# Moving a layer's mixing, transposes and key search to other places in the queues of one core: a streaming encoder step on Trainium2

## The chip, the cores and the metric

The kernel runs on one core of one Trainium2 chip. TensorE (PE) multiplies, VectorE (DVE), ScalarE (ACT) and GpSimd (POOL) work on what it leaves, and SyncE (SP) issues nearly all DMAs from one queue, in order. The metric is the time of one execution in device microseconds.

## What is computed

One layer of a hybrid encoder, for a prompt of 1024 rows and a sample of 32 rows with a cache of 256. Cut to what matters here:

```python
h = rms_norm(x, norm1_g) * (1 + sc1) + sh1
q, k, v, qi, ki, wi, u, vg = jnp.split(h @ w_in, SPLIT_POINTS, axis=-1)
q, k = rope(rms_norm(q, q_norm_g), pos), rope(rms_norm(k, k_norm_g), pos)   # 8 heads x 64
s = jnp.einsum('bqhd,bsd->bqhs', qi, ki)                                     # the indexer
score = jnp.einsum('bqhs,bqh->bqs', jax.nn.relu(s), wi)
score = jnp.where(mask[None], score, -jnp.inf)
top_val, top_idx = lax.top_k(score, topk)       # 256 keys for each query (sample: 72)
...                                             # softmax attention over the chosen keys
u = jax.nn.gelu(u)
vn = layer_norm(jax.nn.gelu(vg), gmlp_ln_g, gmlp_ln_b)
gm = u * (ws_m @ vn + bs)                       # chunks of 128 rows
y = jnp.concatenate([attn, gm], axis=-1) @ w_out
x = x + g1 * y
h2 = rms_norm(x, norm2_g) * (1 + sc2) + sh2
x = x + g2 * (jnp.square(jax.nn.relu(h2 @ w_ff1)) @ w_ff2)
```

## The kernel before

The rows are cut into eight blocks of 128 and one of 32 (the sample, NB). Products are made in three passes over operands split into a rounded part and a rest. The work comes in stages.

First `ada` makes shifts, scales and gates, x is normalised and transposed, and the index columns of w_in are multiplied (`zgroup` with `post_idx`). `score_block` gives each block from 2 on, and the sample, a row of scores for each query.

Then five more column groups of 512 are multiplied, each by one `zgroup`: four pairs of blocks, 48 products of 512 columns (line 313) to a pair, and after each pair a `post_` function. They come in the order q, vg, u, k, v. `post_q` and `post_k` normalise and rotate (`norm_rope`; the rotation, `rope`, is on POOL) and store q and k to DRAM. `post_vg` ends with the mixing product (`mixp`, line 502), which PE reads from a tile that POOL has just written. `post_u` multiplies on POOL and ends with four transposes (`gmt`, line 512). During v, `keys` loads k back and `stack_k` transposes it (`kst`, line 348) and splits it on ACT and DVE. A bank that these steps use comes from a ring of two (`tp`).

Beside these groups runs the search for the 256th largest score of each query (`find_top`): 31 steps, each of which counts the scores above a threshold, bit by bit, and a last part that marks the chosen keys (lines 594 to 610). Two searches are on DVE: `tb` for blocks 2 and 3, `tc` for blocks 5, 4 and NB. Two count on ACT: `ta` for block 7 and `td` for block 6. A step on ACT counts there (line 569), and POOL makes the next threshold in two small operations (lines 570 and 571). All four searches stand in the program before the group v.

`attention` then works on one block at a time, in the order 0, 2, 1, 3, 4, 5, NB, 6, 7. q is loaded from DRAM into `qn` with each head doubled, PE transposes it (`qst`, line 360), and ACT and DVE split it into `qs`. For each head follow the logits (`lgp`, line 690), a DVE operation that adds the mask and takes the minimum (line 691), exp on ACT, a scaling on POOL, transposes (`ppt`) and the product with v (`pv`). After it come w_out (`wo`), the second norm and the feed-forward part (`ff1`, `ff2`), and `emit` stores y, turned by DVE's transposes of 32 x 32 squares, in four DMAs to a piece.

What sets the order: the program is written in the order above, and a scheduler then orders each engine's instructions by simulated times and places tiles in rings. Each engine then runs its queue strictly in that order.

## Time and profile before

| | us |
|---|---|
| median of 3 runs | 1486.31 (1480.2 to 1489.41) |
| the profiled execution | 1479.71 |
| its span, first to last instruction | 1478.0 |
| PE busy | 1380.9 (93%) |
| DVE busy | 843.5 (57%) |
| ACT busy | 528.8 (36%) |
| POOL busy | 550.0 (37%) |

The busy shares are means over stages with different limits, so they say little by themselves. From the trace: the index stage ends near 118 us, attention's first logits start at 469 us, its last product ends near 624 us, the feed-forward part runs from 725 us, and the last product of all ends near 1466 us.

### The profile page before, as it was taken

Reading aid. Unit: us, or ns where it says so; the run is one execution under the profiler, and the core shown is the slowest. Engines: PE = TensorE matmul, PEld = TensorE weight load, DVE = VectorE, ACT = ScalarE, POOL = GpSimd, SP = SyncE. Lnnn points to the kernel's source line nnn. Section 1 sums busy time; section 2 is a strip of 40 time slices with the busy share of each in tenths; the row PEclk is TensorE's granted clock in tenths of the full one; section 3 lists DMA queues with packets and bytes.
Section 4 is the critical chain, followed back from the end, with each engine's and each line's share of the span. In section 5 each row is a group of like instructions: output and inputs, shape, how many; then the busy total and the mean of one; then the engine's idle time right before and its main releaser. Section 6 shows DMA issues by size and latency. Waiting matters only on the chain.

```text
span 1478.0 us, 23705 instructions
## 1 busy us (share of the span) xinstructions
PE 1380.9 (93%) x8792; PEld 1244.5 (84%) x8792; DVE 843.5 (57%) x1987; ACT 528.8 (36%) x1114; POOL 550.0 (37%) x831
## 2 busy tenths in 40 slices
PE   5789797888799999989999999999999999999996
PEld 1767576655467877889999999999999999999996
DVE  1789999999374876532773444334443344433433
ACT  2653346665645765412542111221122211222110
POOL 1656778767950433312342112221122211222120
PEclk9999898999999999999999999999999999999998
DMA  9211111256364221282101111111111111111126
GB/s 363 75 53 47 58 54 51 75 171 234 124 245 115 62 70 64 36 139 73 58 29 49 52 44 44 43 50 51 44 43 44 56 46 44 43 43 57 44 30 89
DMA packets 179947, 114.98 MB, mean 78 GB/s; under 512 B 93412, under 2 KB 147640, under 8 KB 179320
## 3 DMA queue, kind: packets, MB, share of 16 engines
q1 hardware_dynamic: 179832, 113.47, 27.1%
q8 instruction: 69, 1.13, 0.3%
q14 instruction: 46, 0.38, 0.1%
HBM read 97.97 MB, written 15.47 MB: 77 GB/s over the span
## 4 chain that ended last, share of the span: by engine, by line
PE 68%; DVE 17%; POOL 5%; issue 4%; SPq 3%; ACT 2%; DMA 2%; DVEq 0%; POOLq 0%; ACTq 0%
PE f L855 25%; PE f L885 22%; PE wo L836 6%; DVE tcjk L542 4%; PE pv L715 3%; PE lgp L690 3%; PE z L313 3%; PE ppt L702 3%; DVE tbjk L542 2%; SPq L872 2%; POOL tdsm L571 1%; PE ada L154 1%; DVE tcsm L582 1%; DVE sc_b L379 1%; PE qst L360 1%
## 5 line engine op out<-in xcount | busy, mean ns | idle before, releaser
L885 PE MATMUL f<-hid,w 128*128 128x352 f32 x2304 | 372.0, 322 | 0.0
L855 PE MATMUL f<-hh,w 128*128 128x352 f32 x2304 | 371.9, 322 | 0.0
L885 PEld LDWEIGHTS f<-hid,w 128*128 128x128 f32 x2304 | 369.9, 188 | 0.0
L855 PEld LDWEIGHTS f<-hh,w 128*128 128x128 f32 x2304 | 369.1, 188 | 0.0
L775 DVE SCALAR_TENSOR_TENSOR x<-f,mod,x 128x352 f32<-128x352 f32 (+1 forms) x480 | 222.2, 489 | 238.3 <-PE f L885 236.7
L313 PE MATMUL z<-wsp,h 128*128 128x512 f32 (+1 forms) x1152 | 284.0, 397 | 12.9 <-DVE ssh L424 4.4
L860 POOL TENSOR_TENSOR rel<-rel 128x352 f32<-128x352 f32 x96 | 83.6, 872 | 512.4 <-ACT hid L859 512.4
L313 PEld LDWEIGHTS z<-wsp,h 128*128 128x128 f32 x1152 | 213.3, 197 | 71.5 <-issue 12.8
L782 ACT CAST w<-w2r 128x1024 fp32r<-128x1024 f32 x32 | 33.6, 1049 | 283.1 <-PE f L885 272.8
L783 DVE TENSOR_TENSOR w<-w1r,w 128x1024 fp32r<-128x1024 f32 x32 | 39.8, 1245 | 136.3 <-ACT w L782 136.2
L857 ACT ACTIVATE rel<-f 128x352 f32<-128x352 f32 x96 | 44.4, 462 | 153.3 <-PE f L855 152.9
L861 POOL TENSOR_TENSOR hid<-rel,hid 128x352 fp32r<-128x352 f32 x96 | 92.3, 963 | 6.9
L695 POOL TENSOR_SCALAR lg<-lg,ast 128x128 f32<-128x128 f32 (+8 forms) x72 | 51.6, 719 | 97.4 <-DVE ast L694 74.2
L782 ACT CAST w<-w1r 128x1024 fp32r<-128x1024 f32 x32 | 33.5, 1047 | 86.2 <-PE f L855 73.8
L690 PE MATMUL lgp<-kst,qs 128*128 128x256 f32 (+1 forms) x336 | 61.8, 308 | 2.6 <-ACT qs L362 2.5
L195 POOL TENSOR_TENSOR wsp<-wraw,wsp 128x512 fp32r<-128x512 f32 (+1 forms) x44 | 55.5, 1272 | 17.9 <-ACT wsp L194 16.3
L783 DVE TENSOR_TENSOR w<-w2r,w 128x1024 fp32r<-128x1024 f32 x32 | 39.0, 1220 | 37.1 <-ACT w L782 37.1
L692 ACT ACTIVATE lg<-lg,ast 128x128 f32<-128x128 f32 (+8 forms) x72 | 53.9, 750 | 15.3 <-DVE ast L691 10.7
L542 DVE TENSOR_SCALAR_CACHE_REDUCE tcjk<-ya,tcsm 128x768 bf16<-128x768 int16 (+1 forms) x64 | 57.9, 942 | 0.9
L715 PE MATMUL pv<-pT,v 128*64 128x128 f32 (+2 forms) x624 | 57.7, 278 | 0.0
L836 PE MATMUL wo<-gm,wo 128*128 128x352 f32 x288 | 51.9, 329 | 5.1 <-ACT wo L782 5.1
L690 PEld LDWEIGHTS lgp<-kst,qs 128*128 128x128 f32 (+1 forms) x336 | 45.1, 188 | 10.9 <-issue 7.0
(344 smaller groups left out, 1757.5 us busy)
## 6 DMA issues: line engine op xcount, KB each, us to landing
wada<-in_w_ada_dram SPq DMA_DIRECT2D x24, 1024.0 KB, 6.4
w1r<-in_w_ff_dram SPq DMA_DIRECT2D x32, 512.0 KB, 4.0
w2r<-in_w_ff_dram SPq DMA_DIRECT2D x32, 512.0 KB, 3.7
wraw<-in_w_in_dram SPq DMA_DIRECT2D x40, 256.0 KB, 2.9
gm<-gmd SPq DMA_DIRECT2D x4, 1056.0 KB, 5.7
x<-in_x_prompt_dram SPq DMA_DIRECT2D x4, 1024.0 KB, 9.8
gmd<-gmt SPq DMA_DIRECT2D x8, 512.0 KB, 3.6
qn<-qd SPq DMA_DIRECT2D x8, 512.0 KB, 4.7
```

The costliest lines, as they stand in the source:

```text
L313: nc.tensor.matmul(p[:m, :n], h[b][:, k, x, :], w[k][:, y, :], start=k == 0 and q == 0, stop=k == KT - 1 and q == 2)
L542: nc.vector.tensor_scalar(jk[:, :ncol[j]], src, val, None, op0=op, op1=OP.add, accum_out=cnt[:, j:j + 1])
L690: nc.tensor.matmul(ps[:m, d:d + kk.shape[1]], x, kk, start=q == 0, stop=q == 1)
L715: nc.tensor.matmul(ps[64 * j:64 * j + 64, :m], vv, pts[j][:w, k, :m], start=k == 0, stop=k == len(kts) - 1)
L775: nc.vector.scalar_tensor_tensor(y, ps[:, a:a + n], mod[:, 8 * part + k, s:s + 1], y, op0=OP.mult, op1=OP.add)
L782: nc.scalar.copy(ws[:, 0], raw)
L783: eng.tensor_tensor(ws[:, 1], raw, ws[:, 0].bitcast(F32), op=OP.subtract)
L836: nc.tensor.matmul(ps[:, :CW], ws[n][:, x, k, :], mix_at(k, c)[:, y, :], start=k == KO[0] and q == 0, stop=k == KO[-1] and q == 2)
L855: nc.tensor.matmul(ps[:, :CW], ws[n][:, x, k, :], h2_at(k, c)[:, y, :], start=k == 0 and q == 0, stop=k == KT - 1 and q == 2)
L860: nc.gpsimd.tensor_tensor(r, r, r, op=OP.mult)
L861: nc.gpsimd.tensor_tensor(hid[n][:, 1, c * CW:(c + 1) * CW], r, hi.bitcast(F32), op=OP.subtract)
L885: nc.tensor.matmul(ps[:, :CW], w[g][:, x, k, nn * P:(nn + 1) * P], hids[GH * g + k][:, y, c * CW:(c + 1) * CW], start=(g, k) == ks[0] and ...
```

## The change

`zgroup` now keeps a list, `later`. The mixing products, the `gmt` transposes and the key transposes are put on it and made by `settle`, which runs when the products of the next pair are written. The groups come in the order k, q, vg, u, v. After each pair, `advance` lets each search go a given number of steps, held behind the instruction that DVE and ACT had reached two pairs before (in attention: at the block before). The search of blocks 2 and 3 runs in k and q, `tc` starts after k and ends in the group u, and ACT's two searches take 28 of their 31 steps by the end of v and the last 3 in attention. ACT makes its own thresholds, with two small activations instead of POOL's two operations. `norm_rope` squares into SBUF, not in place in the bank.

Attention runs in the order 3, 0, 2, 1, 4, 5, NB, 6, 7. q is loaded by four DMAs in pieces of 32 numbers, so that DVE's transpose of 32 x 32 squares turns it; PE's `qst` transposes are gone. There are four banks for logits and five tiles of them, before three and six. For w_out the weights stand ahead of the rows of x. The last pieces of y use tiles of their own, and every second DMA of theirs goes out from ACT.

```diff
@@ zgroup
+    def settle():
+        while later:
+            later.pop(0)()
...
+    def advance(*pace, back=2):
+        gates.append(gate())
+        g = gates[max(0, len(gates) - back)]
+        with tc.issue_after(g[0]), tc.issue_after(g[1]):
+            for act in (0, 1):
+                for _ in range(pace[act]):
+                    for f in [f for f in searches if f[0] == act][:1 + act]:
+                        if next(f[1], "end") is not None:
+                            searches.remove(f)
...
+            settle()
             post([(b, t0, m, p) for p, (b, t0, m) in zip(ps, g)])
             for b in jobs[j] if jobs else ():
                 keys(b)
+            if pace:
+                advance(*pace[j])
@@ norm_rope, keys, post_vg, post_u
-            nc.scalar.activation(ps[:m], ps[:m], AF.Square)
-            nc.vector.tensor_reduce(ss[:m, e * NH:(e + 1) * NH], heads(ps[:m]), AX.X, OP.add)
+            nc.scalar.activation(t2[:m], ps[:m], AF.Square)
+            nc.vector.tensor_reduce(ss[:m, e * NH:(e + 1) * NH], heads(t2[:m]), AX.X, OP.add)
...
-            stack_k(kt[:, :, d * P:(d + 1) * P], k[d], P, NH)
+            later.append(partial(stack_k, kt[:, :, d * P:(d + 1) * P], k[d], P, NH))
...
+            later.append(partial(mix, b, m, v))
...
+        later.append(partial(gate_out, b, t0, m, x))
@@ find_top
-                        nc.gpsimd.tensor_scalar(dr[:, j:j + 1], cna[:, j:j + 1], ka[:, j:j + 1], 2.0 ** bit, op0=OP.is_lt, op1=OP.mult)
-                        nc.gpsimd.tensor_scalar(t1[:, j:j + 1], t0[:, j:j + 1], dr[:, j:j + 1], -2.0 ** (bit - 1), op0=OP.add, op1=OP.add)
+                        nc.scalar.activation(dr[:, j:j + 1], cna[:, j:j + 1], AF.Sign, bias=ka[:, j:j + 1], scale=-1.0)
+                        nc.scalar.activation(t1[:, j:j + 1], dr[:, j:j + 1], AF.Identity, bias=t0[:, j:j + 1], scale=2.0 ** (bit - 1))
@@ the groups
-    zgroup(zweights(CQ, 512), 512, post_q)
-    zgroup(zweights(CG, 512), 512, post_vg)
-    zgroup(zweights(CU, 512), 512, each(post_u))
...
-    zgroup(wn_, 512, post_k)
...
-    while searches:
-        searches = [f for f in searches if next(f, "end") is None]
+    zgroup(wn_, 512, post_k, pace=4 * ((4, 1),))
...
+    zgroup(wn_, 512, post_q, pace=4 * ((5, 2),))
+    zgroup(zweights(CG, 512), 512, post_vg, pace=4 * ((4, 2),))
+    zgroup(zweights(CU, 512), 512, each(post_u), pace=4 * ((4, 2),))
...
+    zgroup(wv, 512, each(post_v), {0: (4, 0), 1: (1,), 2: (2, 5), 3: (3,)}, pace=((9, 2), (9, 1), (9, 1), (0, 0)))
@@ attention
-        qn = slot([P, D], F32, "qn")
-        nc.sync.dma_start(qn[:m].rearrange("p (a s c) -> p a s c", a=NH, s=2), twice(heads(qd[t0:t0 + m]), m, NH))
+        qn = slot([P, 2, NH, P], F32, "qn")[:, :, :, :m]
+        for q in range(4):
+            d = 32 * (q % 2)
+            nc.sync.dma_start(qn[32 * q:32 * q + 32, 0].rearrange("a h (j b) -> a h j b", b=32), qd[t0:t0 + m].rearrange("(j a) (h c) -> a h j c", a=32, c=HD)[:, :, :, d:d + 32])
...
-        stack_q(qn[:m], m, NH, qs)
+        nc.vector.transpose(qn[:, 1], qn[:, 0])
+        nc.scalar.copy(qs[:, :, 0, :m], qn[:, 1])
+        nc.vector.tensor_tensor(qs[:, :, 1, :m], qn[:, 1], qs[:, :, 0, :m].bitcast(F32), op=OP.subtract)
...
-    for b in (0, 2, 1, 3, 4, 5, NB, 6, 7):
+    for b, pace in ((3, (9, 1)), (0, (9, 1)), (2, (9, 1)), (1, (99, 1)), (4, (0, 2)), (5, (0, 99)), (NB, None), (6, None), (7, None)):
         attention(b)
+        if pace:
+            advance(*pace, back=1)
@@ w_out, emit
+        ws = {n: wsplit(i["w_out"][0, :, n * P:(n + 1) * P], "(k p) c -> p k c", KT, P, "wo", nc.vector if n in (0, 2) else nc.gpsimd) for n in ns}
         for n in ns:
             x_rows(n)
-        ws = {n: wsplit(i["w_out"][0, :, n * P:(n + 1) * P], "(k p) c -> p k c", KT, P, "wo", nc.vector if n in (0, 2) else nc.gpsimd) for n in ns}
...
+            ot = wn.tile([P, CW], F32, name="ot", tag="NS", bufs=2)
...
+            (nc.scalar if q % 2 and c is not None else nc.sync).dma_start(d, s)
```

What PE has queued in the group vg, before, around the mixing products of blocks 2 and 3 (their normalised rows are vg_2092 and vg_2093; h4 to h7 are the inputs of blocks 4 to 7):

```order
L313 MATMUL z_2141<-wsp_1894,h5_446 128x512 x3
L313 MATMUL z_2240<-wsp_1831,h6_471 128x512 x3
L313 MATMUL z_2241<-wsp_1831,h7_496 128x512 x3
L313 MATMUL z_2240<-wsp_1840,h6_471 128x512
L502 MATMUL mixp_2120<-vg_2092,wsT_119 128x128 x4
L502 MATMUL mixp_2131<-vg_2093,wsT_119 128x128 x4
L313 MATMUL z_2240<-wsp_1840,h6_471 128x512 x2
```

And in the changed program, the same two mixing products (now vg_2910 and vg_2911, line 539):

```order
L341 MATMUL z_3121<-wsp_2658,h7_499 128x512 x3
L341 MATMUL z_3120<-wsp_2667,h6_474 128x512 x3
L341 MATMUL z_3121<-wsp_2667,h7_499 128x512
L539 MATMUL mixp_3026<-vg_2910,wsT_122 128x128 x4
L539 MATMUL mixp_3035<-vg_2911,wsT_122 128x128 x4
L341 MATMUL z_3121<-wsp_2667,h7_499 128x512 x2
```

They moved from the first ten products of the pair after the next one to its last eight.

What DVE has queued where attention begins, before (qs is the split q of a block, line 691 the masking of one head's logits, kst the split of the transposed keys):

```order
L353 TENSOR_TENSOR kst_4632<-kst,kst_4632 64x4x128 x4
L363 TENSOR_TENSOR qs<-qst,qs 128x4x128
L691 ISA lg,ast<-lgp,sc_c,rq 128x128
L691 ISA ast 128x1
L691 ISA lg,ast<-lgp,sc_c,rq 128x128
L691 ISA ast 128x1
```

And in the changed program:

```order
L705 STREAM_TRANSPOSE qn<-qn 128x1024
L386 TENSOR_TENSOR kst_4247<-kst,kst_4247 64x4x128 x4
L386 TENSOR_TENSOR kst_4348<-kst,kst_4348 64x4x128 x2
L707 TENSOR_TENSOR qs<-qn,qs 128x8x128
L386 TENSOR_TENSOR kst_4348<-kst,kst_4348 64x4x128 x2
L729 ISA lg,ast<-lgp,sc_b,rq 128x512
L729 ISA ast 128x1
L705 STREAM_TRANSPOSE qn<-qn 128x1024
L729 ISA lg,ast<-lgp,sc_b,rq 128x512
```

The transpose for the second block (the second line 705) now stands behind one masking operation of the first block, and the seven others of that block stand behind it.

What SP has queued behind attention's loads, before (gm are the gated rows, xc the rows of x, wor a third of the weights that `wo` needs first):

```order
L743 DMA gm_6784<-gmd 128x2112
L767 DMA xc<-in_x_prompt_dram 32x32x32 x4
L767 DMA xc<-in_x_sample_dram 32x32 x4
L767 DMA xc<-in_x_prompt_dram 32x32x32 x4
L767 DMA xc<-in_x_sample_dram 32x32 x4
L767 DMA xc<-in_x_prompt_dram 32x32x32 x4
L767 DMA xc<-in_x_sample_dram 32x32 x4
L779 DMA wor<-in_w_out_dram 128x8x128
```

And in the changed program:

```order
L783 DMA gm_6472<-gmd 128x2112
L808 DMA xc<-in_x_prompt_dram 32x32x32 x4
L808 DMA xc<-in_x_sample_dram 32x32 x2
L820 DMA wor<-in_w_out_dram 128x8x128
L808 DMA xc<-in_x_sample_dram 32x32 x2
```

The weights moved from behind 24 loads of x to behind six.

## Rows read from the trace of the kernel before

**Rows 1.** Windows by stage: length, each engine's busy time (instructions), PE clock, DMA.

```profile
118.00:200.00 82.00, 70.78 (x346) 54.37 (x345) 80.07 (x224) 33.97 (x78) 57.18 (x111) 0.94 0.20 63
200.00:280.00 80.00, 67.92 (x360) 54.19 (x359) 74.83 (x198) 47.40 (x120) 61.84 (x141) 0.91 0.17 54
280.00:360.00 80.00, 66.36 (x356) 44.66 (x354) 77.37 (x219) 50.75 (x95) 51.97 (x102) 0.91 0.52 163
360.00:440.00 80.00, 70.58 (x379) 46.45 (x376) 47.43 (x83) 37.65 (x75) 65.10 (x102) 0.91 0.57 196
440.00:469.00 29.00, 25.61 (x130) 20.95 (x128) 12.59 (x21) 13.53 (x25) 0.54 (x4) 1.00 0.32 87
469.00:509.00 40.00, 39.61 (x296) 31.80 (x296) 31.57 (x129) 31.36 (x98) 15.75 (x31) 0.96 0.42 93
509.00:624.00 115.00, 114.96 (x1079) 91.67 (x1078) 80.33 (x259) 65.40 (x162) 37.04 (x43) 1.00 0.21 58
```

**Rows 2.** Chain that ended last, 355 to 470: start, duration, what.

```profile
359.93 8.39 POOL tdsm L571
...
424.65 1.29 DVE tajk L542 x2
...
439.24 1.28 DVE kst L353 x2
...
443.11 6.84 PE z L313 x30
...
469.12 1.34 PE lgp L690 x4
```

**Rows 3.** PE's groups of instructions, 118 to 466: busy, mean ns, idle before.

```profile
L154 PE MATMUL ada<-wada,silu 128*32 128x512 f32 x128 | 20.2, 705 | 0.0
...
L502 PE MATMUL mixp<-vg,wsT 128*128 128x128 f32 (+1 forms) x72 | 14.0, 361 | 10.2 <-POOL vg L497 10.2
...
L348 PE MATMUL kst<-ident,kr 128*128 128x128 f32 (+1 forms) x44 | 6.1, 277 | 1.8 <-DVE kst L353 1.0 <-DMA kr<-out_dram 0.8
```

**Rows 4.** DVE's and POOL's groups of instructions, 118 to 469.

```profile
L428 DVE TENSOR_TENSOR kz<-kz 128x512 f32<-128x512 f32 (+1 forms) x9 | 8.5, 949 | 19.5 <-POOL kz L285 19.5
...
L571 POOL TENSOR_SCALAR tdsm<-tdsm 128x1 f32<-128x1 f32 x31 | 19.2, 620 | 1.8
...
L570 POOL TENSOR_SCALAR tdsm<-tdsm 128x1 f32<-128x1 f32 x31 | 13.4, 431 | 5.1 <-ACT tdajk L569 3.8
```

**Rows 5.** Line 582 (search step on DVE): ns min/median/max, first and last start.

```profile
L582 DVE TENSOR_TENSOR tcsm<-tcsm x31: 129/163/1222, 240.1 to 353.9; 128x3 f32<-128x3 f32 x31
```

**Rows 6.** Chain that ended last, 600 to 645, PE at work in attention.

```profile
606.41 1.15 PE lgp L690 x8
...
612.02 1.14 PE ppt L702 x8
613.16 1.02 PE pv L715 x16
```

**Rows 7.** PE's transposes of q in attention, 466 to 624.

```profile
L360 PE MATMUL qst<-ident,qn 128*128 128x128 f32 x64 | 10.2, 284 | 0.2 <-DVE qs L363 0.2
```

**Rows 8.** DMAs of qn (the tile's view), in pieces of 256 bytes: issue to landing.

```profile
DMA to landing us min/median/max: 4.4/4.7/5.1
```

**Rows 9.** DMAs of xc, in pieces of 128 bytes: issue to landing.

```profile
DMA to landing us min/median/max: 1.6/3.3/6.1
```

**Rows 10.** SP's queue where attention ends, timeline: start, duration, four issues of xc.

```profile
607.60 2.16 SPq L767 DMA_DIRECT2D xc<-in_x_prompt_dram  x4
```

**Rows 11.** Splitting w_out (the tile's view), on tiles of 128x1024.

```profile
L782 ACT CAST wo<-wor x8: 1032/1049/1055, 620.7 to 684.9; 128x1024 fp32r<-128x1024 f32 x8
...
L783 DVE TENSOR_TENSOR wo<-wor,wo x2: 1214/1220/1226, 622.7 to 636.9; 128x1024 fp32r<-128x1024 f32 x2
```

**Rows 12.** PE where w_out begins: timeline, in brackets the idle time before.

```profile
636.91 3.87 PE L836 MATMUL wo<-gm,wo 128*128 128x352 f32 x14 [5.11 <-ACT wo L782]
```

**Rows 13.** The end: timeline of SP's queue and of DVE.

```profile
1429.18 46.91 SPq L872 DMA_DIRECT2D out_dram<-ot  x72
...
1460.47 1.28 DVE L868 STREAM_TRANSPOSE ot<-x 128x1056 f32<-128x1056 f32 x1
...
1471.67 0.55 DVE L868 STREAM_TRANSPOSE ot<-x 128x352 f32<-128x352 f32 x1 [5.45 <-DMA out_dram<-ot]
```

More of the change, by code (lines that the diff above doesn't have):

```diff
@@ L1 @@
 from contextlib import ExitStack
+from functools import partial
 import numpy as np
@@ L293, in hybrid_step, with gate, zgroup @@
     PASSES = ((0, 0), (0, 1), (1, 0))
-    def zgroup(wp, n, post, jobs=None):
+    searches = []
+    gates = []
+    later = []
+    def settle():
+        while later:
+            later.pop(0)()
+    def gate():
+        seen = nc.cur_bb.bb.instructions
+        return [next(x for x in reversed(seen) if x.engine == e) for e in (nc.vector.engine, nc.scalar.engine)]
+    def advance(*pace, back=2):
[7 more added lines that the diff above has]
+                            searches.remove(f)
+    def zgroup(wp, n, post, jobs=None, pace=None):
         w, pt = wp
@@ L757, in squares, with turned @@
         return [t[:, n * P + 32 * q:n * P + 32 * q + 32].rearrange("(j a) b -> a j b", a=32) for q in range(4)]
-    def quarter(t, q):
-        return t[32 * q:32 * q + 32].rearrange("a (j b) -> a j b", b=32)
+    def turned(t):
+        return [t[32 * q:32 * q + 32].rearrange("a (j b) -> a j b", b=32) for q in range(4)]
     def x_rows(n):
@@ L765, in x_rows @@
         for t, src in ((x[:, 0:T], i["x_prompt"][0]), (x[:, T:NT], i["x_sample"][0])):
-            for q, s in enumerate(squares(src, n)):
-                nc.sync.dma_start(quarter(t, q), s)
+            for d, s in zip(turned(t), squares(src, n)):
+                nc.sync.dma_start(d, s)
         nc.vector.transpose(xk(n, 0, NT), x)
@@ L793, in norm2 @@
     def norm2(c):
-        acc = wn.tile([P, CW], F32, name="acc", tag="NA", bufs=3)
+        acc = wn.tile([P, CW], F32, name="acc", tag="NA", bufs=2)
         for k in range(KT):
@@ L800, in norm2 @@
             else:
[L801 removed]
+                sq = wn.tile([P, CW], F32, name="sq", tag="NS", bufs=2)
                 nc.scalar.activation(sq, x, AF.Square)
@@ L864, in emit @@
     def emit(n, c=None):
-        t0, t1 = (0, NT) if c is None else (c * CW, (c + 1) * CW)
-        ot = (wf if n % 2 else wr).tile([P, NT], F32, name="ot", tag="XC" if n % 2 else "OT", bufs=2 if n % 2 else 1)[:, :t1 - t0]
-        nc.vector.transpose(ot, xk(n, t0, t1 - t0))
-        parts = [(ot[:, :min(t1, T) - t0], o[0][0, t0:min(t1, T)])] + ([(ot[:, T - t0:], o[1][0])] if t1 > T else [])
-        for src, dst in parts:
-            for q, d in enumerate(squares(dst, n)):
-                nc.sync.dma_start(d, quarter(src, q))
+        if c is None:
+            t0, t1 = 0, NT
+            ot = (wf if n % 2 else wr).tile([P, NT], F32, name="ot", tag="XC" if n % 2 else "OT", bufs=2 if n % 2 else 1)
+        else:
+            t0, t1 = c * CW, (c + 1) * CW
+            ot = wn.tile([P, CW], F32, name="ot", tag="NS", bufs=2)
+        nc.vector.transpose(ot, xk(n, t0, t1 - t0))
+        e = min(t1, T)
+        for q, (d, s) in enumerate(zip(squares(o[0][0, t0:e], n), turned(ot[:, :e - t0]))):
+            (nc.scalar if q % 2 and c is not None else nc.sync).dma_start(d, s)
+        if t1 > T:
+            for q, (d, s) in enumerate(zip(squares(o[1][0], n), turned(ot[:, T - t0:]))):
+                (nc.scalar if q % 2 and c is not None else nc.sync).dma_start(d, s)
     def ff2(gs):
```

69 lines of the change are left out of this document (36 added, 33 removed).

## The prediction

> **What bounds the kernel now.** I read the windows by stage first [rows 1]. From 469 us to the end of attention PE is busy nearly all the time (39.6 of 40, then 114.96 of 115), so a microsecond taken off PE's own path there is worth a microsecond. From 118 to 469 PE is busy for 70.78 + 67.92 + 66.36 + 70.58 + 25.61 = 301 of 351 us and so waits for 50; its clock there is 0.91 to 1.00 of full speed. The engine that is full is DVE: 80.07 of 82, 74.83 of 80, 77.37 of 80, that is 232.3 of 242 or 96%. Only from 360 to 440 does it fall to 47.4 of 80.
>
> The chain that ended last says why the stage still lasts until 469 [rows 2]. Near 360 it runs over POOL's thresholds for ACT's searches, at 424.65 over DVE's last part of the search `ta`, at 439.24 over DVE's split of the transposed keys, and from 443.11 PE has products of v left. So DVE's queue is followed by a tail on PE, and attention starts at 469.12. The groups tell where DVE waits in that last stretch [rows 4]: the split of k's rotated rows waited 19.5 us for POOL, whose thresholds cost 19.2 + 13.4 us for one search alone.
>
> **The stage of the groups and searches.** The stage ends when PE has V's last transposed keys and its last products, and these stand behind DVE's split of the sample's keys, which in the changed DVE queue stands behind the search `tc`. So I count DVE's work ahead of that point. Before it did 80.07 + 74.83 + 77.37 + 47.43 = 279.7 us up to 440 [rows 1]. Of this the last parts of ACT's searches, which run on DVE from 424.65 to 439.24 [rows 2], move into attention: 14.6 off, 265 left. Nothing large is added; the squares go to SBUF, and the reduction reads as many numbers. K comes first now, so its wait for POOL is no longer at the end, and POOL has lost the threshold operations, 32.6 us for each of two searches, less the three late steps.
>
> How full DVE will be is a choice. It was 96% in the three full windows and 279.7/322 = 87% over all four. The gates of `advance` make bubbles of their own, so I take the middle, 92%: 265/0.92 = 288 us, until 406. After that point the order gives PE 120 products of v at 6.84/30 = 0.228 [rows 2], 27.4 us; 17 products of `ada` at 20.2/128 = 0.158, 2.7; 12 transposes of it and 32 of keys at 6.1/44 = 0.139 [rows 3], 6.1. Together 36 us, until 442, and one more for the last split: first logits at 443 against 469, **-26**.
>
> The mixing products' wait for POOL, 10.2 us [rows 3], and the transposes behind the next pair lie inside this: while DVE is the bound, a wait of PE that goes only makes PE wait elsewhere. Were DVE not the bound, they would be what lets PE reach its floor, 118 + 301 = 419, or -50. DVE at 96% gives 276 + 37 = 431, -38. If K's wait of 19.5 appears again, wherever it stands, the gain is 26 - 19.5, some -6; if the gates take the rest, nothing. The term runs from -50 to +2.
>
> **Attention.** PE loses the 64 transposes of q, **-10.2** [rows 7], all on a full PE. In their place each block has four DMAs, a transpose on DVE, a copy on ACT and a subtraction on DVE. DVE (31.6 of 40, 80.3 of 115) and ACT (31.4 of 40, 65.4 of 115) have room in the mean [rows 1], also for the 14.6 us of search parts and ACT's six late steps. The order of one block against the next is what may cost. By their tiles all blocks but the last share one `qn` in the changed program, before there were two. So a block's load is issued when the subtraction of the block before has ended, and each refill is a chain: four issues by SP 2.2 [rows 10], landing 4.8, DVE's transpose 1.3, as one of a like size took [rows 13], ACT's copy 1.05, subtraction 1.2 [rows 11]: 10.6 us. No row shows the landing; loads of q in pieces of 256 bytes took 4.4 to 5.1 [rows 8], loads in pieces of 128, as now, 1.6 to 6.1 [rows 9], so I take the first's median, rounded up, as the same bytes move, and the ends 10.1 and 11.8 for the chain.
>
> Against it stands what PE has queued between two blocks' first logits: for block 3 to 0, 32 logits at 1.15/8 = 0.144 and four `ppt` at 0.14 [rows 6], 5.2 us; 0 to 2 about 10.5, 2 to 1 about 8, 1 to 4 about 8.5, by the same prices; each later one 11 or more. The stalls are 5.4 + 0.1 + 2.6 + 2.1 = 10, and 2 for the second block's transpose, which stands ahead of seven maskings on DVE, so that these wait for a DMA and PE for their exps. So +12 against -10.2: **+2**, from -10 (loads that land in time) to +5 (chain of 11.8).
>
> On SP's queue nothing urgent stands behind these loads until `gm`.
>
> A rule on the load speaks against the change. The trace has loads of 128-byte pieces no slower than those of 256 [rows 8, 9], though smaller ones in bytes. The Trainium skill, DMA: Bandwidth & Descriptors, section Why small descriptors are slow (HBM only), says that each packet costs some cycles besides those for its bytes, so that halves of 256 bytes cost about 1.27 times as much per byte. By that, as an estimate, the landing would be 6.0 instead of 4.8, the four stalls 15 instead of 10, and the sum 5 us less of a gain; no run here shows it for this load.
>
> **Start of w_out.** PE waited 5.11 us there for ACT's cast [rows 12], which waits for weights behind 24 loads; now they are behind six. 18 issues at 2.16/4 = 0.54 [rows 10] are 9.7 us, more than the wait. **-5** (0 if ACT is what is late, as its casts take 1.05 each [rows 11]).
>
> **Feed-forward.** Untouched; 0.
>
> **The end.** SP's 72 issues of y take 46.9 us in a row, and DVE's last transpose waited 5.45 for a tile that they hold [rows 13]. Own tiles and issues from ACT take that away; the last DMA's own landing stays: **-3** (-1 to -5.45).
>
> **Sum.** -26 + 2 - 5 - 3 = -32. The profiled execution took 1479.7 us, 1.7 more than its span; this gives 1447.7. The median of the runs, 1486.3, is 6.6 above that execution, so on the runs' footing **1454**.
>
> **The rivals.**
>
> *DVE gets quicker, PE becomes the bound.* A step of the search on DVE took 163 ns in the median and 1222 at most [rows 5], so something else held some of them; POOL, with fewer operations, may hold it less. The Trainium skill, SBUF — State Buffer, section Who interferes with whom, says that a DVE operation with two inputs in SBUF and a POOL operation that reads SBUF shut each other out; the spread in the row agrees, without naming the cause. DVE may then end some 20 us earlier, near the floor: -49 for the stage, in the sum -55, or 1431; since some of DVE's work is its own, I put this case at 1437. Against it: 232 of 242 us full is mostly long operations. Chance 0.16.
>
> *The change does not do what it says.* The gates and DVE's strict order hold the searches where they were: a group's `post_` operation stands behind a search step that waits for its gate, and PE's banks behind that. The stage stays at its length (0 to +2), attention +2, w_out -5, the end -3: 1476 profiled, or 1482. For it: DVE's queue was full before and all its work but 14.6 us stays. Chance 0.17.
>
> *Slower: the single `qn`.* Each microsecond of the refill chain above 10.6 costs four over the first four refills, later ones once it exceeds their cover of 11 to 20. It eats the whole gain of 32 at 10.6 + 8 = 18.6, a landing of 12.8 us. With a landing of 16 the chain is 22: stalls 16.8 + 11.5 + 14 + 13.5 = 56 and 17 at later blocks, with 2 for the maskings 75, less 10.2: attention +65, and with -26 - 5 - 3 the sum is +31, 1517. For it: four times the issues, and twice the packets for the same bytes. Against it: 6.1 was the most that any load of such pieces took [rows 9]. Chance 0.09.
>
> **How the numbers follow.** Forecast 0.58, PE's floor 0.16, no change 0.17, slower 0.09. A measurement of this kernel tells about 1%, 15 us, from no change. The forecast's own range follows from DVE at 96% (-38) to 87% (265/0.87 = 305, first logits at 460, -9): 1442 to 1471, all faster by over 1%. The range must leave out at most 0.2: the slower case (0.09), and the lower part of the floor's case; it goes from 1430 to 1481, into the middle of no change. Faster: 0.58 + 0.16 less a little for the forecast's upper edge, 0.73; same 0.18; slower 0.09.
>
> **What would show it.** Right: first logits near 443; DVE over 90% busy from 118 to 400; no wait of PE for the mixing's input; PE idle some 2 to 6 us before the first logits of blocks 0, 2, 1 and 4, ended by `qs`; no wait where w_out begins; the last transposes of y without a wait for a DMA. Wrong: PE fully busy from 118 to 440 (then the floor held), a new wait of DVE on SP's loads in attention longer than 10 us (then the single tile), or DVE at 80% with first logits near 465 (then the gates). Most exposed is the 92%: 4 points are 12 us.

## The result, and the profile after

The changed kernel took 1471.93 us (median of 7 runs, 1468.36 to 1475.93), the kernel before 1484.26 beside it (7 runs, 1479.66 to 1489.41): a ratio of 0.9912, with a 95% interval from 0.989 to 0.9934. It is faster by 0.9%, inside the range, but I had forecast 2.2%. The profiled executions took 1479.7 and 1471.4, their spans are 1478.0 and 1469.5.

The marks of each stage, from the timeline of PE (first logits, first product of w_out, first of the feed-forward part, end of the last) and the span, say where the forecast failed:

| us | before | after | change | forecast |
|---|---|---|---|---|
| start to first logits | 469.1 | 446.4 | -22.7 | -26 |
| attention, to the first product of w_out | 154.7 | 173.2 | +18.4 | +2 |
| w_out | 101.2 | 96.4 | -4.8 | -5 |
| feed-forward | 740.4 | 740.9 | +0.5 | 0 |
| last product to the end | 12.5 | 12.6 | +0.1 | -3 |
| sum | 1478.0 | 1469.5 | -8.5 | -32 |

Four of the five came out within 4 us; attention gave back most of what the groups had gained.

The windows of the kernel after in the stage of the groups (length, then busy time of PE, its weight loads, DVE, ACT and POOL, PE's clock, share and rate of DMA):

```profile
118.00:200.00 82.00, 78.93 (x386) 61.01 (x385) 77.01 (x178) 34.26 (x74) 66.69 (x100) 0.96 0.20 62
200.00:280.00 80.00, 66.16 (x351) 46.02 (x349) 76.08 (x200) 54.36 (x143) 59.26 (x105) 0.95 0.34 111
280.00:360.00 80.00, 72.75 (x380) 58.49 (x381) 75.14 (x192) 38.03 (x108) 43.96 (x94) 0.92 0.22 68
360.00:400.00 40.00, 31.55 (x199) 19.07 (x198) 37.54 (x104) 30.99 (x81) 15.59 (x21) 0.87 0.79 255
400.00:440.00 40.00, 40.00 (x209) 28.83 (x208) 24.02 (x42) 27.66 (x65) 3.02 (x11) 1.00 0.62 203
```

DVE did 77.01 + 76.08 + 75.14 + 37.54 = 265.8 us by 400 (265 were counted until 406), 94% of the 282. From 360 to 400 it has no hole any more; from 400 to 440 PE is full. PE's last wait for DVE in this stage ends at 394.8, and DVE's last split of the sample's own keys (`kstn`) at 402.9 (timelines of PE and DVE):

```profile
394.77 0.43 PE L381 MATMUL kst<-ident,kr 32*128 32x32 f32 x4 [1.50 <-DVE gmt L556]
```

```profile
402.57 0.29 DVE L386 TENSOR_TENSOR kstn<-kst,kstn 64x128 fp32r<-64x128 f32 x1
```

The wait of 19.5 us for POOL in K's step [rows 4] is 1.3 in the kernel after (groups of instructions; busy, mean ns, idle before it):

```profile
L462 DVE TENSOR_TENSOR kz<-kz 128x512 f32<-128x512 f32 (+1 forms) x9 | 7.7, 859 | 1.3 <-POOL kz L288 1.3
```

Attention, in the same view and columns:

```profile
446.40:460.00 13.60, 8.99 (x38) 8.20 (x38) 8.94 (x20) 7.51 (x15) 1.76 (x3) 0.51 0.48 96
...
500.00:510.00 10.00, 10.00 (x82) 7.79 (x82) 10.00 (x45) 7.25 (x20) 4.02 (x6) 1.00 0.09 16
510.00:520.00 10.00, 8.54 (x72) 6.31 (x72) 10.00 (x27) 4.40 (x10) 4.70 (x3) 1.00 0.36 52
520.00:530.00 10.00, 9.28 (x72) 6.63 (x69) 10.00 (x30) 5.10 (x13) 3.88 (x5) 1.00 0.01 2
530.00:540.00 10.00, 7.01 (x66) 4.73 (x64) 10.00 (x22) 5.48 (x11) 2.90 (x3) 0.94 0.12 20
540.00:550.00 10.00, 10.00 (x80) 6.91 (x77) 5.88 (x18) 3.95 (x13) 4.85 (x6) 0.71 0.81 252
550.00:560.00 10.00, 10.00 (x96) 7.75 (x95) 6.79 (x26) 5.35 (x22) 2.58 (x6) 0.97 0.59 218
560.00:570.00 10.00, 10.00 (x51) 8.36 (x50) 5.33 (x20) 3.89 (x12) 2.02 (x2) 0.50 0.00 0
570.00:580.00 10.00, 10.00 (x72) 9.14 (x70) 5.25 (x19) 4.89 (x10) 3.26 (x4) 0.68 0.01 2
```

Two things are to be seen: PE is idle in places where before it hardly was, and its clock is at the lower of its two levels (0.50, that is 1.2 GHz) at three places: at the start, near 540, and from 560 to 576, where PE has no idle time at all. To size both in every run I cut attention into windows of 2 us and took the idle time (length less busy time) and the clock loss (busy time times what the granted clock lacks to 1); what is left is PE's work at the full clock. Before: 152.7 of work, 0.3 idle, 1.7 clock. After: 144.5, 12.3 and 16.4. So of the +18.4, -8.2 is the work of the transposes, +12.0 idle time and +14.7 clock.

The first idle stretch, in the chain that ended last in the kernel after (start, duration, what):

```profile
446.29 1.24 DVE qs L707
448.17 0.68 SPq L700
448.90 0.76 SPq L700
449.70 3.83 DMA qn<-qd
453.65 1.25 DVE qn L705
455.60 2.93 PE lgp L728 x12
```

This is the refill of the single tile of q: the subtraction of block 3 releases it at 447.5, four loads follow, and DVE's transpose waits for them. The timelines of DVE and PE in the same place (in brackets the idle time before and what ended it) show who waits behind it:

```profile
453.65 1.25 DVE L705 STREAM_TRANSPOSE qn<-qn 128x1024 f32<-128x1024 f32 x1 [3.64 <-DMA qn<-qd]
```

```profile
455.60 2.93 PE L728 MATMUL lgp<-kst,qs 128*128 128x256 f32 x12 [3.60 <-DVE ast L729]
```

PE waits for a masking that stands behind that transpose in DVE's queue. In the whole stage PE waited 7.8 us for maskings, 3.6 here and 3.7 where DVE was full from 500 to 540, and for the split q of any block but the first only 0.55 (PE's waits for `lgp`; us, times, longest; the 1.7 lie ahead of the first logits):

```profile
PE lgp L728 <- DVE ast L729: 7.8, 7, 3.6
PE lgp L728 <- ACT qs L706: 1.7, 1, 1.7
PE lgp L728 <- DVE qs L707: 1.4, 2, 0.8
```

From subtraction to subtraction the refill took 11 us (10.6 forecast), though the loads themselves landed sooner than I had taken: 3.4 us in the median, 3.7 at most, against 4.7 for the loads of 256-byte pieces [rows 8]. By the Trainium skill, DMA: Bandwidth & Descriptors, section Why small descriptors are slow (HBM only), they would have come later, at 6.0 by my estimate. The measured 3.4 is less, but each of the four loads carries a quarter of the bytes, which the estimate left out; so these rows do not test the cost of a packet. From the first issue to the last landing the four took 6.0 us here (447.5 to 453.5), where I had taken 2.2 + 4.8.

Where w_out begins the 5.11 us of [rows 12] are down to two waits of 0.38 and 1.00. At the end the last transpose waits as before, 6.89 where it was 5.45 [rows 13] (timelines of PE, DVE and SP after):

```profile
627.90 1.24 PE L877 MATMUL wo<-gm,wo 128*128 128x352 f32 x6 [0.38 <-ACT wo L823]
630.14 1.87 PE L877 MATMUL wo<-gm,wo 128*128 128x352 f32 x10 [1.00 <-DVE wo L824]
```

```profile
1464.54 0.55 DVE L914 STREAM_TRANSPOSE ot<-x 128x352 f32<-128x352 f32 x1 [6.89 <-DMA out_dram<-ot]
1465.98 0.93 SPq L920 DMA_DIRECT2D out_dram<-ot  x2
```

### The profile page after: what moved, and what is told of

It reads as the page before. It is cut to its first block, busy times and chain, and to the rows that moved or that the text cites. A ratio compares the mean times of both kernels' runs of the same rounds, so it can differ in the third digit from the quotient of the medians.

```text
span 1469.5 us, 23531 instructions
## 1 busy us (share of the span) xinstructions
PE 1379.6 (94%) x8720; PEld 1244.0 (85%) x8720; DVE 861.7 (59%) x1971; ACT 549.4 (37%) x1237; POOL 508.8 (35%) x708
## 4 chain that ended last, share of the span: by engine, by line
PE 66%; DVE 10%; issue 2%; ACT 1%; DMA 1%; POOL 1%; SPq 1%; DVEq 0%; POOLq 0%; ACTq 0%
PE f L933 25%; PE f L897 23%; PE wo L877 5%; DVE scrap L579 4%; PE lgp L728 3%; PE z L341 3%; PE pv L753 3%; PE ppt L740 2%; DVE hh L865 1%; DVE lg L729 1%; DVE hf L863 1%; PE ada L157 1%; DMA out_dram<-ot 0%; PE kst L381 0%; DVE tcsm L620 0%
## 5 line engine op out<-in xcount | busy, mean ns | idle before, releaser
L816 DVE SCALAR_TENSOR_TENSOR x<-f,mod,x 128x352 f32<-128x352 f32 x480 | 222.2, 489 | 238.3 <-PE f L933 236.7
L341 PE MATMUL z<-wsp,h 128*128 128x512 f32 (+1 forms) x1152 | 282.0, 396 | 11.3 <-POOL wsp L198 6.7
L733 POOL TENSOR_SCALAR lg<-lg,ast 128x512 f32<-128x512 f32 (+8 forms) x72 | 55.8, 782 | 104.6 <-DVE ast L732 74.0
L728 PE MATMUL lgp<-kst,qs 128*128 128x256 f32 (+1 forms) x336 | 67.9, 335 | 11.1 <-DVE ast L729 7.8
L728 PEld LDWEIGHTS lgp<-kst,qs 128*128 128x128 f32 (+1 forms) x336 | 51.0, 215 | 20.6 <-DVE ast L729 11.0
L198 POOL TENSOR_TENSOR wsp<-wraw,wsp 128x512 fp32r<-128x512 f32 (+1 forms) x44 | 56.4, 1290 | 20.5 <-ACT wsp L197 14.1
L579 DVE TENSOR_SCALAR_CACHE_REDUCE scrap<-ya,tcsm 128x768 bf16<-128x768 int16 (+1 forms) x64 | 60.4, 944 | 1.9
L730 ACT ACTIVATE lg<-lg,ast 128x512 f32<-128x512 f32 (+8 forms) x72 | 53.8, 748 | 16.6 <-DVE ast L729 13.0
L740 PE MATMUL ppt<-ident,lg 128*128 128x128 f32 (+2 forms) x312 | 53.5, 287 | 2.3 <-DVE pT L743 1.0
```

The lines of the kernel that those rows point to most:

```text
L341: nc.tensor.matmul(p[:m, :n], h[b][:, k, x, :], w[k][:, y, :], start=k == 0 and q == 0, stop=k == KT - 1 and q == 2)
L579: nc.vector.tensor_scalar(jk[:, :ncol[j]], src, val, None, op0=op, op1=OP.add, accum_out=cnt[:, j:j + 1])
L728: nc.tensor.matmul(ps[:m, d:d + kk.shape[1]], x, kk, start=q == 0, stop=q == 1)
L740: nc.tensor.transpose(pt[:w, (k - c) * P:(k - c) * P + m], lg[:m, k * P:k * P + w], ident[:m, :m])
L816: nc.vector.scalar_tensor_tensor(y, ps[:, a:a + n], mod[:, 8 * part + k, s:s + 1], y, op0=OP.mult, op1=OP.add)
```

## The experiments

Seventeen runs. The texts ahead of each name four explanations of what attention lost: theory F, the last search parts on DVE; theory Q, the single tile of q; theory S, the sample's small products, which let PE's clock fall; and rival D, that the clock answers late to PE's idle time. In the table every line is a profiled execution, taken apart as above; the time is the median of the timed runs, and the ratio to the kernel before beside them is given where there are several ("one" marks a single run). The column "fall" says whether the clock fell by the sample's products.

| run | first logits | attention | work | idle | clock | fall | time | ratio, 95% |
|---|---|---|---|---|---|---|---|---|
| before | 469.1 | 154.7 | 152.7 | 0.3 | 1.7 | no | 1484.3 | 1 |
| after | 446.4 | 173.2 | 144.5 | 12.3 | 16.4 | yes | 1471.9 | 0.989 to 0.993 |
| e1 searches end with v | 455.6 | 167.0 | 144.6 | 11.3 | 11.0 | yes | 1475.6 | 0.993 to 0.997 |
| e2 two loads of q | 453.3 | 176.6 | 143.1 | 16.2 | 17.3 | yes | 1476.2 | 0.994 to 0.998 |
| e3 both | 461.3 | 156.5 | 142.3 | 2.7 | 11.5 | yes | 1470.9 | 0.990 to 0.995 |
| e4 q on PE | 446.7 | 157.3 | 150.6 | 5.0 | 1.7 | no | 1460.3 | 0.983 to 0.988 |
| e5 transposes added | 448.4 | 172.6 | 146.2 | 14.6 | 11.8 | yes | 1470.0 | 0.988 to 0.993 |
| e6 sample later | 453.8 | 168.5 | 145.4 | 12.2 | 10.9 | moved | 1473.4 | one |
| e7 no list | 446.9 | 171.8 | 145.1 | 15.2 | 11.5 | yes | 1473.5 | 0.991 to 0.996 |
| e8 e4 and the end | 446.8 | 157.3 | 150.6 | 4.9 | 1.7 | no | 1456.7 | 0.980 to 0.988 |
| e9 products added | 450.8 | 181.9 | 163.8 | 14.1 | 4.0 | no | 1481.8 | 0.996 to 1.000 |
| e10 thresholds on POOL | 448.7 | 162.2 | 146.6 | 12.8 | 2.8 | no | 1462.4 | one |
| e11 before, weights first | 466.7 | 160.6 | 151.6 | 0.5 | 8.5 | yes | 1475.8 | one |
| e12 e8 and e1 | 455.9 | 162.7 | 150.2 | 2.7 | 9.8 | yes | 1466.8 | 0.984 to 0.995 |
| e13 after again | 450.0 | 169.8 | 145.9 | 11.8 | 12.2 | yes | 1470.6 | one |
| e14 before again | 467.0 | 154.8 | 152.7 | 0.3 | 1.7 | no | 1477.5 | one |
| e15 halves of q's tile | 449.7 | 165.0 | 145.7 | 7.7 | 11.6 | yes | 1467.0 | 0.989 to 0.993 |
| e16 k last | 448.6 | 172.7 | 144.6 | 13.8 | 14.4 | yes | 1471.5 | 0.993 to 0.997 |
| e17 no pace | 462.0 | 163.7 | 144.3 | 9.2 | 10.1 | yes | 1477.2 | one |

The kernel before had medians from 1479 to 1486 beside these runs, so medians of runs that were not made side by side compare to some 5 us. First logits are one execution's as well: in nine profiles of kernels that differ in attention or behind it alone (after, e2, e4, e5, e6, e8, e9, e13, e15) they came between 446.4 and 453.8, 449.5 in the mean, and in the three with the stage of before at 466.7 to 469.1, 467.6 in the mean. So the stage brought some 18 us rather than 22.7, and one profile that differs from that mean by less than some 4 us tells nothing.

**e1: the searches end with v.**

```diff
-    zgroup(zweights(CU, 512), 512, each(post_u), pace=4 * ((4, 2),))
+    zgroup(zweights(CU, 512), 512, each(post_u), pace=4 * ((4, 3),))
-    zgroup(wv, ..., pace=((9, 2), (9, 1), (9, 1), (0, 0)))
+    zgroup(wv, ..., pace=((9, 1), (9, 1), (9, 1), (0, 1)))
```

> The changed kernel with one edit: ScalarE's two searches take three steps a pair in the group u, so that all 31 steps and their last parts on DVE are made by the end of v, and none in attention. In the changed kernel attention took 173.2 us from its first logits (446.4) to the first product of w_out (619.6), 18.4 more than before. Theory F, the last search parts on DVE in attention (14.6 us, where DVE is full from 500 to 540 and PE's clock is low from 540 to 580) are most of it: attention 156 to 160 us, clock near 1.0 after 480, first logits 446 to 454, time 1458 to 1465. Theory Q, the single tile of q's loads is most of it: attention 168 or more, time 1468 or more, since the loads stay as they are.

Attention 167.0, 6.2 less, but the first logits came at 455.6, 6 us behind the mean of the nine, since DVE then makes the last search parts in front of the transposed keys (busy 19.45 of 20 us from 440 to 460). Of the 6.2 in attention 1.0 is idle time and 5.4 clock, so theory F is not most of it.

**e2: two loads of q alternate.** The turned copy takes a tile of the ring of the logits, as memory has no room for another.

```diff
-        qn = slot([P, 2, NH, P], F32, "qn")[:, :, :, :m]
+        qn = qns[:, len(qdone) % 2, :, :m]
...
-        nc.vector.transpose(qn[:, 1], qn[:, 0])
+        qt = wa.tile([P, T], F32, name="qt", tag="LG", bufs=5).rearrange("p (a c) -> p a c", a=NH)[:, :, :m]
+        nc.vector.transpose(qt, qn)
```

> The changed kernel with q's tile split into two loads that alternate, and the turned copy in a tile of the ring of the logits (five, as they are); the late search steps stay. Theory Q: the wait of 3.6 us for the second block's load, the low clock of 0.51 in the first 14 us of attention and the small waits behind later loads go, attention 162 to 165 us, time 1461 to 1464. Theory F: attention 169 to 173, time 1468 to 1472; the gap from 510 to 580 stays. If the turned copies crowd the ring of the logits, attention is longer than 173.

DVE no longer waits for any load of q, but idle time rose to 16.2, in many waits of PE for DVE, ACT and POOL alike, as expected if the ring is crowded. For theory Q it tells nothing.

**e3: both, the turned copy in the searches' scratch tile.**

> Both edits together: ScalarE's searches end with v, two loads of q alternate, and the turned copy of q lies in the searches' scratch tile, which is free by then. Theories F and Q both real and apart: attention near 150 us (PE's own work is 144 at full clock, as before's 154.5 less 10.5), time 1450 to 1457. If only F is real it equals the first edit alone, if only Q the second alone.

With the searches out of attention in both, two loads take the idle time from 11.3 (e1) to 2.7. The first logits are late, because the first transpose now waits for the scratch tile (PE waits 10.4 us there), so a part of that idle time has only moved ahead of attention: it ends at 617.8, after 622.6 in e1 and 619.6 in the change. Idle time in attention is as low as was expected of both together; the clock loss of 11.5 was not expected, and 7 of it lies behind 20 us in which PE was idle for half a microsecond.

**e4: q turned on PE, as before.**

```diff
-        qn = slot([P, 2, NH, P], F32, "qn")[:, :, :, :m]
-        for q in range(4):
-            ...
+        qn = slot([P, D], F32, "qn")
+        nc.sync.dma_start(qn[:m].rearrange("p (a s c) -> p a s c", a=NH, s=2), twice(heads(qd[t0:t0 + m]), m, NH))
...
-        nc.vector.transpose(qn[:, 1], qn[:, 0])
-        ...
+        stack_q(qn[:m], m, NH, qs)
```

> The changed kernel with q's way as before: loads in pieces of 256 bytes into tiles of their own, PE's transposes (10.5 us) through one bank, three banks for logits. Theory Q: what the loads cost comes back and pays for the transposes, attention 168 to 174, first 14 us of it at a clock over 0.8. Theory F: attention 178 to 184, as the search parts still hold DVE, and the transposes lie on PE's path on top. The time 1467 to 1473 by Q, 1476 to 1483 by F.

Better than either theory: attention 157.3 and the best time until then, 11.6 us under the change by the medians and 9 by the ratios, with the late search parts still there; the two intervals of the ratio do not touch. PE does 6.1 us more work and saves 7.3 of idle time and 14.7 of clock. So most of what attention lost, it lost to the way of q over DVE. The profiled execution took 1453.7, less than the median of 1460.3, so in others the clock may have given back less.

**e5 and e9: larger work on PE by the sample's products.** e5 has the first edit (transposes for blocks 6 and 7), e9 the second; both have three banks for logits instead of four.

```diff
+        for c in (0, 4) if b in (6, 7) else ():
+            fl = bank("fil", "Q", 1)
+            for a in range(4):
+                nc.tensor.transpose(fl[:, a * P:(a + 1) * P], qn[:, 0, c + a], ident)
```

```diff
+            for f in range(4) if b == NB else ():
+                nc.tensor.matmul(bank("fil", "Q", 1)[:m], pts[f % 2][:, f // 2, :m], v_sb[0][:, f], start=True, stop=True)
```

> The changed kernel plus sixteen transposes of q on PE for blocks 6 and 7, whose results nobody reads (and three banks for logits instead of four, for their bank); they fall into the sample's block. In the changed kernel PE had no idle time from 540 to 580, yet its granted clock was 0.50 from 560 to 576, behind the sample's products of 32 columns; in the kernel before and in the run with q turned on PE, where transposes lie among them, it stayed at 1.00. Theory S, the small products alone let the clock fall and the transposes held it: clock 1.0 from 560 to 576, attention 173 - 8.5 + 2.5 = 167 us, time 1466. Rival D, the fall is a late answer to the idle time at 510 to 540: clock still 0.5 there, attention 175, time 1474.

> The changed kernel plus sixteen products of 512 columns on PE in the sample's block, four to a pair of heads, that take the sample's weights and so stand among its products of 32 columns; nobody reads their results (three banks for logits instead of four, for their bank). The transposes of the run before this one had ended 9 us ahead of the first of these products, so it could not tell. Theory S, PE's clock falls because the sample's small products stand without larger work among them: clock 1.00 from 560 to 580, clock loss in attention 16.4 - 8.5 = 8 us, against some 4 us of added products: attention 167 to 171. Rival D, the idle time ahead of it lets the clock fall: 0.50 for some 14 us there all the same, attention 175 to 178.

e5 could not tell: its transposes ended at 546, the sample's own transposes of 32 rows and its products with v, which I call its small products, begin at 554.5, and the clock fell at 561. In e9 the added products lie among them and the clock stayed at 1.00. PE's windows of 4 us in e3, then PE's windows of 5 us in e9 (length, PE's busy time, clock, DMA):

```profile
552.00:556.00 4.00, 4.00 (x45) 1.00 0.80 260
556.00:560.00 4.00, 4.00 (x42) 0.99 0.04 15
560.00:564.00 4.00, 4.00 (x20) 0.50 0.00 0
564.00:568.00 4.00, 4.00 (x22) 0.50 0.00 0
568.00:572.00 4.00, 4.00 (x25) 0.50 0.00 0
572.00:576.00 4.00, 4.00 (x27) 0.80 0.00 0
```

```profile
560.00:565.00 5.00, 5.00 (x32) 1.00 0.92 375
565.00:570.00 5.00, 5.00 (x32) 1.00 0.09 35
570.00:575.00 5.00, 5.00 (x23) 1.00 0.00 0
575.00:580.00 5.00, 5.00 (x32) 1.00 0.00 0
```

In both PE is busy throughout. So no idle time lies directly ahead of the low clock of e3. That larger products hold the clock rests on this one profile of e9, and one without any added work (e10, below) kept its clock too, so it is supported and not shown. The three banks do not explain it, since the clock fell in e5. The added products cost 19 us, not 4: each is two instructions of 605 ns, so this is no cure.

**e6: the sample's block between 6 and 7.** One line of the order of blocks.

> The changed kernel with the sample's block between blocks 6 and 7 instead of between 5 and 6. Theory S: the 14 to 16 us at clock 0.5 move with it, to about 585 to 605, or spread if more of the products of 7 lie among them; attention 168 to 175. Rival D: the low stretch stays near 560 to 576 as the idle time of 510 to 540 stays, whatever PE does then.

The clock stayed at 1.00 from 560 to 580 and was at the low level from 590 to 601: the fall moved with the sample, as theory S has it, though PE's idle time stayed at 520 to 533. Together with e3 and e9 this speaks against rival D.

**e7: no list.** `later` calls each step at once.

> The changed kernel without the list: mixing products, gated transposes and key transposes are made at once, as before. If DVE bounds the groups, as I forecast (DVE busy 266 of 282 us from 118 to 400), PE's waits for POOL are beside it: first logits 446 to 450, time 1471 to 1475. If the delay is what brought the stage 22.7 us, the waits come back (10 us for the mixing's input) and key transposes hold PE in v: first logits 456 to 469, time 1481 to 1494.

First logits 446.9, time 1473.5. The delay of the list brought nothing that can be told. The wait for POOL that it was to take away was not gone with it either: PE waited 6.5 us for the mixing's input in the kernel after, against 10.2 before [rows 3] and 8.0 in e7 (groups of the kernel after).

```profile
L539 PE MATMUL mixp<-vg,wsT 128*128 128x128 f32 (+1 forms) x72 | 11.4, 314 | 6.5 <-POOL vg L531 6.5
```

**e8: the last piece of y in another ring, on top of e4.**

```diff
-            ot = wn.tile([P, CW], F32, name="ot", tag="NS", bufs=2)
+            ot = wn.tile([P, CW], F32, name="ot", tag="NS" if c < 2 else "NH", bufs=2)
```

> The run with q turned on PE, plus one edit at the end: the last of the three pieces of y uses a tile of another ring, so that its transpose no longer waits 6.9 us for the DMAs of the first piece. If that wait ends the kernel: 3 to 6 us less than the run without it, 1454 to 1457. If the queue of DMAs on SP does, whose issues run to the end anyway: 0 to 1 us less, 1459 to 1460.

The last transpose starts without a wait, but the span is only 1.0 shorter than e4's: SP's issues go on for 7.6 us behind it (timelines of DVE and SP in e8).

```profile
1441.35 0.55 DVE L913 STREAM_TRANSPOSE ot<-x 128x352 f32<-128x352 f32 x1
```

```profile
1441.67 3.34 SPq L919 DMA_DIRECT2D out_dram<-ot  x4
1445.10 2.92 SPq L916 DMA_DIRECT2D out_dram<-ot  x6
1448.07 0.92 SPq L919 DMA_DIRECT2D out_dram<-ot  x2
```

The medians differ by 3.6, less than their spread, so the end is not shown to bring anything. It has the lowest median of all, 1.6% under the kernel before. Its four runs go from 1452.7 us at a granted clock of 0.981 over the whole span to 1465.5 at 0.965, and the profile is that of the 1452.7: that the clock did not fall by the sample holds for this execution, and may not hold for the others.

**e10: thresholds on POOL.** The two activations are POOL's two operations again.

> The changed kernel with the thresholds of ScalarE's searches made by POOL's two operations again, as before. If POOL's load and its hold on DVE's operations was what delayed the groups: first logits 455 to 465 instead of 446, DVE's busy time from 118 to 400 up from 266, with longer steps of the search. If the order of the groups and the last search parts are what brought the 22.7 us: first logits 445 to 450.

First logits 448.7, as with the change. The longest of DVE's comparisons of counts took 1642 ns here, 1242 in the change and 1251 before (1222 in the search of [rows 5]), so they are stretched without POOL's thresholds too. The time is low because PE's clock hardly fell in attention in this one execution (2.8 lost instead of 16.4); whether the thresholds have a part in that is not shown.

**e11: the kernel before with the weights ahead of the rows of x.**

> The kernel before with one edit: the weights for w_out are loaded ahead of the rows of x. As I forecast: PE's wait of 5.1 us where w_out begins goes, from its first product to the first of the feed-forward part 96 us instead of 101.2, the rest as before. If ACT's casts are late and not the weights: 101 as before.

From its first product to the feed-forward part w_out took 94.5 (101.2): -6.7, so the whole of that term is the order of these loads. This run also showed the clock's fall with q turned on PE.

**e12: e8 with the searches ended in v.**

> The run with q turned on PE and the tile of another ring at the end, plus ScalarE's searches ended with v, so that no search work is in attention. In the changed kernel that edit made the first logits 9.2 us later and attention 6.2 us shorter. With q on PE attention has only 5.0 us of idle time and 1.7 of clock loss left. Theory F dead: attention 152 to 156, first logits 454 to 457, time 5 to 8 us longer than without the edit, 1461 to 1465. If the late search parts still cost what they did beside DVE's turning: attention 150, time 1457 or less.

First logits at 455.9, 6 us behind the mean of the nine as in e1, and idle time in attention only 2.2 less: with q on PE the late search parts are mostly hidden beside it, as forecast, and by these two profiles letting them go late gains some 4 us. Attention was longer for the clock alone, which fell by the sample in this execution.

**e13 and e14: both kernels again, unchanged.**

> The changed kernel, unchanged, for a second profile. If the fall of PE's clock behind the sample's block belongs to the change: 0.50 from about 560 to 576 again, attention 171 to 175 us. If it comes and goes between executions: some executions of it, perhaps this one, have a clock of 1.00 there and 163 to 167 us, and the kernel before has it at times.

> The kernel before, unchanged, for a second profile. In its first one the clock stayed at 1.00 behind the sample's block, attention 154.7 us, time 1479.7; its runs lie between 1477 and 1490. If the fall belongs to the change: 1.00 again and 154 to 156. If it comes and goes: either that, or 0.50 for 8 to 16 us from about 572, attention 159 to 163 and a time of 1485 or more.

Each repeated itself: the fall in the changed kernel, none in the one before. Over all profiles, the clock fell by the sample in 11 of 12 with q turned on DVE and no large products added (all but e10), and in 2 of 6 with q turned on PE (e11, e12). So the fall is frequent with q turned on DVE, but it comes without that too, and is missing once with it.

**e15: the halves of q's tile freed apart.**

```diff
-        qn = slot([P, 2, NH, P], F32, "qn")[:, :, :, :m]
+        qn = qn1[:, :, :, :m]
```

`qn1` is made once, ahead of the blocks.

> The changed kernel with q's tile made once, so that the next block's load waits for DVE's transpose alone, which reads the half it fills, and no longer for ACT's copy and DVE's subtraction of the other half. Theory Q: the refill chain of 10 us is 2.3 shorter and starts 2.3 earlier, four of them in the first blocks: idle time in attention 12 - 6 = 6 us or less, attention 165 to 169 with the same clock. If DVE's own work and the late search parts are what PE waits for: idle time 10 to 13 as before, attention 171 to 175.

Idle time 7.7, attention 165.0 (e13, made beside it, has 11.8 and 169.8). In the view of the tile DVE waited 4.6 us for loads of q, in the change 8.8, of which some 3 each lie ahead of attention (us, times; the first line is the change, the second e15):

```profile
  DMA qn<-qd: 8.8, 6
```

```profile
  DMA qn<-qd: 4.6, 3
```

So some 4 of the 12 us of idle time are the single tile's, by one profile; the ratio of the runs, 0.9913, is that of the change, so the times do not show it.

**e16: k as the last group but one, as before.**

> The changed kernel with the groups in the order of before, q, vg, u, k, v, and the same steps of the searches in the same places of that row. If the order is what brought the stage the larger part of its 22.7 us: first logits 455 to 465, DVE less busy from 360 to 440 as it waits for POOL's rotation of k, time 1478 to 1488. If not: first logits 444 to 450, time 1469 to 1475.

First logits 448.6, as with the change: the order of the groups is not what brought the stage its gain.

**e17: no pace.** All four searches stand ahead of v as before.

> The changed kernel without the pace: all four searches stand in the program before the group v, step by step in turn as before, and end before attention; the order of the groups, the delayed steps, ScalarE's thresholds and q's way stay as changed. If the pace and the last search parts are what brought the stage 22.7 us: first logits 464 to 470, as before, and DVE with some 30 us idle between 360 and 440. If only the last search parts count, as when they alone were moved back: first logits 454 to 458. Attention as with the searches ended early, 160 to 168 us.

First logits 462.0, 12.5 behind the mean of the nine: pace and late search parts together are 12.5 of the stage's 18 us, and by e1 and e12 the late parts are 6 of them, which leaves some 6 for the pace, by one profile. DVE was not idle from 360 to 440, as I had expected, but busy 78.3 of 80 us: it had done less before, and search work was still ahead of the keys.

## Why the prediction failed, step by step

**The stage of the groups** was right in that DVE was the bound at first and PE's tail the rest, and near in size: -22.7 in the two profiles, -18 by the means of nine and three, against -26. But the hand-over was not where I had put it, and two errors met. PE waited for DVE only until 394.8, not 406, and the search `tc`, which I had counted ahead of the sample's keys, made its last part behind their split (401.8 to 414.1); that 265.8 us of DVE's work by 400 equal the 265 counted is luck. PE's tail was longer in turn: 48 us without a gap instead of 36, and 3.7 more for the last key transposes and waits. Nor did the sign of no wait for the mixing's input appear: 6.5 us of it stayed, as it may while DVE is the bound. The rivals that moved this term are out: PE is not at its floor of 419, and the gates did not hold the stage at its length. Of the parts, the late search parts (e1, e12) and, by one profile, the pace (e17) matter; list, thresholds and order alone are not shown to (e7, e10, e16).

**Attention is the step that failed**: +18.4 for the +2 of the sum, and the term that I did not have is PE's clock. I counted a wait of PE as costing its own length, and the work that is left as running at the clock of before, so that the clock stood at nothing, without a reason. It cost 14.7 more in this profile: 2.8 at the start (4.5 against 1.7), 3.3 at the idle stretch that ends at 539, and 8.5 by the sample. In the second profile of the same kernel (e13) it cost 10.5 more.

The idle time was forecast as 12 and came as 12.0, but that is luck: the stalls of 10 us at the first logits of blocks 0, 2, 1 and 4, ended by `qs`, came as 0.55, and the waits for maskings, taken as 2, came as 7.8. The transposes' work was forecast as 10.2 and came as 8.2.

The first two losses go with waits. The clock was low from 446.7, behind a wait of 1.71 us, through the wait of 3.60, until 460; and it fell again in a wait of 2.47 (timeline of PE after):

```profile
446.40 0.35 PE L728 MATMUL lgp<-kst,qs 128*128 128x256 f32 x1 [1.71 <-ACT qs L706]
539.14 0.63 PE L728 MATMUL lgp<-kst,qs 128*32 128x256 f32 x2 [2.47 <-DVE ast L729]
```

That waits let the clock fall is what the Trainium skill, TensorE: Matmul & The Clock Gate, section HAM oscillation — how this bites in real kernels, says of waits for DMAs; these two rows agree, with waits for ACT and DVE. The third loss lies behind no wait: it went with the sample's block (e6) and was not there with larger products among the small ones (one profile, e9), so I take the small products for the likely cause. I took the transposes of q as 10.2 us of mere cost. Whether it was they that held the clock among the small products is not shown, as it fell with them there in e11 and e12. What the whole way of q over DVE cost is shown by e4: 9 to 12 us of the runs' time.

**w_out** was right (-4.8; e11 alone -6.7). **The end** was wrong by 3: the transpose's wait was on no path that ends last, since SP's queue is in issue until 2 to 3 us before the end in any case (e8). **The footing** added 6.6 to both kernels; the spans of the profiles differ by 8.5 and the medians by 12.3. **The slower rival**, a slow load into the single tile, had the right place and the wrong price: the loads landed in 3.4.

What stays open: why the clock fell in e11 and e12 but not in e4, e8 and e10; the rest of attention's idle time, of which the single tile alone explains 4 us (e15) and the late search parts alone 1 (e1); and the last 5 us of the stage's gain (18 less 12.5), which no run isolated.

## What to carry to other kernels

Work taken from a busy TensorE is worth its length only if the engine's clock stays up afterwards: read the granted clock beside the busy time, and give it a term of its own in the sum. Here 10.2 us of transposes went and 10 to 15 us of clock were lost with them. Before an operation that waits for a DMA is put on an in-order engine, see who is queued behind it, and how many tiles the load has. Work that shares a queue with the steps towards the next stage can be let go late, if that stage has room for it.

## What the runs showed of the hardware

TensorE's clock went to its lower level while the engine was busy without a gap, in 13 of the 19 profiles, each time 4 to 12 us behind the first of the sample's transposes of 32 rows, for 10 to 17 us. Each of the four loads of 128-byte pieces, a quarter of the tile, landed 3.4 us after its issue in the median (kernel after), where one load of the whole tile in pieces of 256 bytes took 4.7 (before), but SP spent 0.68 us on the issue of each.
